# Gate recurrence between the two heads of the first attention; selection by step sums, one comparison per block, low halves split on VectorE

## The chip, the cores and the metric

The kernel runs on one core of one Trainium2 chip. The metric is the device time of one execution in microseconds (us): before the change 1979.73 us, the median of three runs (1979.67 to 1980.06). Lower is better.

Of a core's engines the kernel uses TensorE (PE: matmuls and transposes, with its weight loads as a queue of their own), VectorE (DVE), ScalarE (ACT), GpSimd (POOL) and SyncE (SP, which here only starts DMAs). Each engine takes its instructions strictly in the order in which they stand in its queue, and waits where an operand is not ready.

## What is computed

One decoder block over 512 tokens of width 1024, in float32. A normalised input goes through one combined projection. Two token mixers read it, a differential attention and an mLSTM with 8 heads each; their outputs are gated, merged and projected. Then comes a feed-forward part in which each token picks 128 of 16384 experts. Cut to what the change touches:

```python
# mLSTM: log-gates, running sums and running maxima over the tokens
log_f = log_sigmoid(f_pre);  b = cumsum(log_f);  Dm = b_j - b_k + i_k
m_j = max(max(Dm), b + m_prev);  W = exp(Dm - m_j)

# expert choice, for each token and each of 8 heads
s = einsum('thpd,hpnd->thpn', (h @ w_q), sub_keys)      # two halves of 128 scores
v_top, i_top = top_k(s, 16)
cand     = v_top[0][:, None] + v_top[1][None, :]        # sums of two scores
cand_idx = i_top[0][:, None] * 128 + i_top[1][None, :]
sc, sel  = top_k(cand, 16)
idx  = take_along_axis(cand_idx, sel)                   # expert = n1 * 128 + n2
gate = softmax(sc)

# experts
act = gelu(einsum('thed,td->the', U[idx], h))
y   = einsum('the,thed->td', gate * act, V[idx])
```

## The kernel before

A float32 product is made of three matmuls on halves: `hi` is a rounded copy (a cast, mostly on ACT), `lo` what is left over (a subtraction, `split` at L138, or L181 for the weights of a projection).

**Head pairs, about 60 to 600 us.** The loop at L667 takes the heads in four pairs `hp`. For each it calls `attention` (projections of q, k and v; then for each of the two heads `u` the scores `sc` L478 to L481, the maximum `nmx` L483, the exponential L487, `p` L492, the transposes `aTp` L495, their split, the output `po` and its transposes `pt` L507, and the scaled result `mrg` L509), then `mlstm`, then three gate projections `om`, `gm` and `ga`, each closed by sigmoids on ACT (L682). PE projects `om`, `gm` and `ga` with matmuls of 256 columns (L187 to L189). The first pair alone also calls `gate_chain`, the recurrence over the gates of all heads: on an 8-partition tile four rounds of a running maximum `M` (L349), `mprev`, `iw` and `R` (L350 to L352), then exponentials on ACT (L355 to L357), splits, and transposes `RTp` (L369). It reads two small projections made long before, and the mLSTM of every pair reads its results.

**Routing and the dense weights, about 640 to 1013 us.** `scores(h)` projects the keys of a head and takes the best 16 of each half on VectorE. `select` (called by `select_dense` with four heads of one of three token blocks, six calls, and by two later `select_gather` calls for a fourth token block) adds up to 50 candidate sums `cand` on VectorE and their indices `cidx` on GpSimd, takes the best 16, and then finds the index of each with, per head, a comparison `eq` on VectorE (L797), a product `oh` on GpSimd (L799) and a sum on VectorE (L800), over 16x50 elements. `slots` (L816) turns the indices and gates of a token block. `build_w` (L833) makes the dense gate weights of 384 tokens in 48 blocks of 8 tokens: two comparisons `onehot` (`e2`, `e1`), two products `gated` (`r_hi`, `r_lo`), each of 128x1024 fp16 (L844), on VectorE, save 6 of the 48 `r_lo`, which are on GpSimd; then 16 small matmuls into `wps` (L852, L853).

Meanwhile PE is given the first products with `U`: `up(n1)` (L961) loads a row of 128 experts, casts `hi_U` on ACT (L966), subtracts `lo_U` (L967; for n1 below 35 on GpSimd, later on VectorE), copies one column of `lo_U` on GpSimd (`pace`, L969, to pace the gathers), and issues 24 matmuls `act` (L975 to L977) and a gelu into one of 32 `ga` tiles.

**Main loop, 1013 to 1984 us.** For each of 128 rows n1: one further `up`, a load of `V` and its split, the gate weights, and 18 matmuls `y` (L1021).

The order on each engine is not the order of the code: a scheduler goes through all instructions with durations of its own and hands each engine a list. So where code is moved, the lists move around it.

Of the kernel before, what the change touches and what calls it, by code (L numbers as in the profile page):

```python
# [61 lines left out]
def block_kernel(ctx: ExitStack, tc: tile.TileContext, a, out, dbg=None):  # L62
# [709 lines left out]
    def select(vals, inds, n, mk, didx, dgate):  # L772

        fi = mk("fi", [P, 2, n, TOPK])
        A.activation(fi[:, 0], inds[:, 0], AF.Copy, scale=float(KEYS))
        A.copy(fi[:, 1], inds[:, 1])
        cand = mk("cand", [P, n, NC])
        cidx = mk("cidx", [P, n, NC])
        for eng, dst, src in ((V, cand, vals), (G, cidx, fi)):
            off = 0  # L780
            for i in range(8):
                m = PAIRS[i]
                eng.tensor_tensor(dst[:, :, off:off + m], src[:, 1, :, 0:m],
                                bc(src[:, 0, :, i:i + 1], [P, n, m]), op=OP.add)
                off += m
            eng.tensor_tensor(dst[:, :, off:off + 8], src[:, 0, :, 8:16],
                            bc(src[:, 1, :, 0:1], [P, n, 8]), op=OP.add)
# [21 lines left out]
    def mk_rp(name, shape, dt=F32):  # L809
        return rp.tile(shape, dt, tag=name, bufs=2, name=name)  # L810

    def select_dense(t, h0, n):
        hs = slice(h0, h0 + n)
        select(vals[t][:, :, hs], inds[t][:, :, hs], n, mk_rp, idxf[t][:, hs], gates[t][:, hs])

    def slots(t):  # L816
# [9 lines left out]
        pair = [P, P, 2]  # L826
        V.tensor_copy(n1T[:, cs], bc(ii[:, 1, :, None], pair))
        V.tensor_copy(n2T[:, cs], bc(ii[:, 2, :, None], pair))
        gp = bc(ps[:, P:2 * P, None], pair)
# [89 lines left out]
    def select_gather(h0):  # L919
# [5 lines left out]
        def mk(name, shape, dt=F32):  # L925
            n = int(np.prod(shape[1:])) * (2 if dt == F16 else 4) // 4
            if name in ("oh", "eq"):
# [1 line left out]
            elif name in ("cand", "cidx"):
                t_, n0 = s0, 256 * (name == "cidx")  # L930
# [178 lines left out]
```

## Time and profile before

| What | us |
|---|---|
| median of three runs | 1979.73 |
| profiled execution, its own time | 1986.29 |
| span of that execution's instructions | 1984.2 |
| busy PE / DVE / ACT / POOL | 1826.5 / 1465.3 / 806.8 / 861.2 |

The profiled execution is 6.6 us longer than the median, and 2.1 us of its own time lie outside its span. A busy time is the sum over an engine's instructions; an engine that waits within an instruction for a resource counts as busy. In a timeline, the bracket behind a row gives the idle time ahead of it and what ended it. An instruction's duration may overlap the next one's start by some 0.08 us.

### The profile page before, as it was taken

How to read it: one execution, taken by the hardware profiler on the slowest of the kernel's cores; microseconds unless marked ns; L12 is line 12 of the kernel's file. 1: busy time of each engine (PE TensorE's matmuls, PEld its weight loads, DVE VectorE, ACT ScalarE, POOL GpSimd, SP SyncE). 2: the span in 40 equal slices, each digit the busy share in tenths (PEclk: the TensorE clock that was granted, in tenths of full speed). 3: DMA queues.
4: the chain of work that ended last, by engine and by line, in shares of the span. 5: the costliest groups of instructions: out<-in, count | busy, mean ns of one | idle time of the engine just before them, and what ended most of it. 6: DMA issues, size and time to landing. Idle time of an engine off the chain costs nothing.

```text
span 1984.2 us, 29045 instructions
## 1 busy us (share of the span) xinstructions
PE 1826.5 (92%) x10748; PEld 1648.0 (83%) x10748; DVE 1465.3 (74%) x2740; ACT 806.8 (41%) x1361; POOL 861.2 (43%) x721
## 2 busy tenths in 40 slices
PE   5989999899997988778899989999999999999997
PEld 4979899798986877678888778889988888888986
DVE  7653646546557799998999878888777677767777
ACT  4545464464553323344444333333333333332332
POOL 2513425234234256675533556555433423333433
PEclk8999999999998999899899999999999999999998
DMA  7321414324223222255596699999978888887983
GB/s 278 123 64 60 149 65 154 113 67 139 64 86 107 86 90 81 85 183 202 203 312 215 216 331 339 334 345 348 337 253 296 293 283 291 288 299 234 320 290 129
DMA packets 160284, 404.27 MB, mean 204 GB/s; under 512 B 14471, under 2 KB 63368, under 8 KB 160142
## 3 DMA queue, kind: packets, MB, share of 16 engines
q1 hardware_dynamic: 117026, 240.91, 37.2%
q0 software_dynamic: 36864, 134.23, 18.6%
q10 hardware_dynamic: 6252, 27.28, 3.6%
q8 instruction: 84, 1.38, 0.3%
q14 instruction: 58, 0.48, 0.1%
HBM read 373.52 MB, written 28.84 MB: 203 GB/s over the span
## 4 chain that ended last, share of the span: by engine, by line
PE 51%; DVE 23%; DMA 10%; issue 6%; POOL 5%; ACT 4%; SPq 0%; DVEq 0%; POOLq 0%; ACTq 0%
PE y L1021 18%; PE act L977 5%; PE act L975 5%; PE act L976 5%; DMA ada_w<-ada_w 4%; DMA gath<-V,idx 3%; DVE onehot L844 3%; DVE gated L844 2%; DVE lo_V L138 1%; DVE lo_U L967 1%; DVE eq L797 1%; DMA gath<-U,idx 1%; POOL gath L901 1%; DVE idxf L800 1%; ACT hi_U L966 1%
## 5 line engine op out<-in xcount | busy, mean ns | idle before, releaser
L977 PE MATMUL act<-h_hi,lo_U 128*128 128x384 f32 x1024 | 353.9, 346 | 14.7 <-POOL lo_U L967 9.7
L975 PE MATMUL act<-h_hi,hi_U 128*128 128x384 f32 x1024 | 351.5, 343 | 1.9 <-ACT ga L979 1.9
L976 PE MATMUL act<-h_lo,hi_U 128*128 128x384 f32 x1024 | 350.7, 342 | 0.0
L917 DVE SCALAR_TENSOR_TENSOR yg<-gath,act,yg 128x1024 f32<-128x1024 f32 x127 | 162.9, 1283 | 110.3 <-DMA gath<-V,idx 109.6
L1021 PE MATMUL y<-lo_V,ahi 128*128 128x512 f32 x762 | 238.9, 394 | 5.5 <-DVE lo_V L138 5.5
L1021 PE MATMUL y<-hi_V,alo 128*128 128x512 f32 x762 | 234.1, 394 | 4.0 <-DVE alo L138 4.0
L1021 PE MATMUL y<-hi_V,ahi 128*128 128x512 f32 x762 | 222.1, 396 | 7.3 <-ACT hi_V L137 7.3
L901 POOL DMA_INDIRECT gath<-U,idx x128 | 176.6, 1380 | 115.3 <-DVE junk L907 101.1
L137 ACT CAST hi_V<-raw_V 128x1024 fp32r<-128x1024 f32 x128 | 134.1, 1051 | 225.6 <-PE y L1021 197.1
L977 PEld LDWEIGHTS act<-h_hi,lo_U 128*128 128x128 f32 x1024 | 197.0, 192 | 22.4 <-POOL lo_U L967 11.1
L969 POOL COPY pace<-lo_U 128x1 f32<-128x1 f32 x128 | 69.9, 548 | 331.6 <-DVE lo_U L967 330.1
L975 PEld LDWEIGHTS act<-h_hi,hi_U 128*128 128x128 f32 x1024 | 197.8, 193 | 10.8 <-ACT ga L979 3.1
L976 PEld LDWEIGHTS act<-h_lo,hi_U 128*128 128x128 f32 x1024 | 197.5, 193 | 3.6
L137 ACT CAST ahi<-ga 128x384 fp32r<-128x384 f32 x127 | 65.1, 513 | 302.2 <-DVE ga L1006 152.1
L138 DVE TENSOR_TENSOR lo_V<-raw_V,hi_V 128x1024 fp32r<-128x1024 f32 x128 | 158.0, 1236 | 33.2 <-ACT hi_V L137 30.6
L966 ACT CAST hi_U<-raw_U 128x1024 fp32r<-128x1024 f32 x128 | 134.1, 1048 | 110.0 <-PE act L976 92.3
L1021 PEld LDWEIGHTS y<-hi_V,alo 128*128 128x128 f32 x762 | 143.5, 189 | 35.9 <-DVE alo L138 5.2
L1021 PEld LDWEIGHTS y<-lo_V,ahi 128*128 128x128 f32 x762 | 142.7, 189 | 36.7 <-DVE lo_V L138 7.9
L1021 PEld LDWEIGHTS y<-hi_V,ahi 128*128 128x128 f32 x762 | 143.0, 190 | 32.1 <-ACT hi_V L137 8.0
L901 POOL DMA_INDIRECT gath<-V,idx x128 | 152.5, 1192 | 38.0 <-issue 30.2
L907 DVE SCALAR_TENSOR_TENSOR junk<-gath,hrow 128x1024 bf16<-128x1024 f32 x128 | 156.1, 1220 | 11.9 <-DMA gath<-U,idx 11.2
L967 POOL TENSOR_TENSOR lo_U<-raw_U,hi_U 128x1024 fp32r<-128x1024 f32 x35 | 105.0, 3001 | 72.5 <-ACT hi_U L966 59.1
(461 smaller groups left out, 4413.1 us busy)
## 6 DMA issues: line engine op xcount, KB each, us to landing
raw_U<-UT SPq DMA_DIRECT2D x128, 512.0 KB, 5.1
raw_V<-V SPq DMA_DIRECT2D x128, 512.0 KB, 5.0
ada_w<-ada_w SPq DMA_DIRECT2D x96, 256.0 KB, 4.0
W_dram<-st ACTq DMA_DIRECT2D x24, 960.0 KB, 4.5
W<-W_dram SPq DMA_DIRECT2D x60, 384.0 KB, 10.4
raw_wq<-wq SPq DMA_DIRECT2D x16, 512.0 KB, 3.5
raw_q<-w_in SPq DMA_DIRECT2D x8, 512.0 KB, 4.9
raw_k<-w_in SPq DMA_DIRECT2D x8, 512.0 KB, 3.6
```

The lines of the kernel that those rows point to most:

```text
L137: A.copy(hi, src)
L138: eng.tensor_tensor(lo, src, hi.bitcast(F32), op=OP.subtract)
L844: eng.tensor_tensor(dst.rearrange("p t (n u) -> p t n u", u=2), x.rearrange("p t (n u) -> p t n u", u=2), bc(y[:, b * TB:(b + 1) * TB, Non ...
L901: G.indirect_dma_start(out=t_, out_offset=None, in_=src, in_offset=bass.IndirectOffsetOnAxis(ap=idx0[:, s:s + 1], axis=0))
L907: V.scalar_tensor_tensor(junk2, u, 1.0, hrow, op0=OP.mult, op1=OP.mult, accum_out=act[:, s:s + 1])
L917: V.scalar_tensor_tensor(yg, v, act[:, s:s + 1], yg, op0=OP.mult, op1=OP.add)
L966: A.copy(hi, raw)
L967: (G if n1 < NGA + 3 else V).tensor_tensor(lo, raw, hi.bitcast(F32), op=OP.subtract)
L975: T.matmul(ps, hi[:, ks], h_hi[:, k], start=(k == 0), stop=False)
L976: T.matmul(ps, hi[:, ks], h_lo[:, k], start=False, stop=False)
L977: T.matmul(ps, lo[:, ks], h_hi[:, k], start=False, stop=(k == KD - 1))
L1021: T.matmul(ys[d][j], l[:, tsl], r[:, j * 512:(j + 1) * 512], start=(m == 0 and i == 0), stop=(m == KEYS - 1 and i == 2))
```

## The change

- `gate_chain` is called between head 0 and head 1 of the first pair's attention, no longer after both.
- `select` makes no index table and does nothing on GpSimd. The position of a pick is compared with the 16 offsets at which the rows of candidates start (`ge`, is-greater-or-equal, four heads at once, 1024 elements); that is multiplied by the steps of the first index (`di`) and by the steps of the offsets (`doff_c`) into the two halves of `stp`; one sum over 2048 elements gives the first index and the row's offset. The rest of the position is compared with 0 to 15 and multiplied by the second index, and summed (1024 elements). All of it is on VectorE, so a call has five elementwise operations of 1024 fp16 elements, two sums, and four small operations, where it had four comparisons and four sums on VectorE and four products on GpSimd.
- `slots` turns three tables and needs no shift or mask.
- `build_w` makes both comparisons of a block in one operation of 2048 elements, and all 48 `r_lo` are on VectorE.
- `lo_U` is on VectorE for all n1. The `pace` copy stays on GpSimd.
- The tables off_c and doff_c are filled by 32 GpSimd memsets of one column each; the two `select_gather` calls use the new `select`.

```diff
-PLO = 1
...
-    def attention(hp, y, ssq):
+    def attention(hp, y, ssq, between=None):
...
+            if u and between:
+                between()
...
-        attention(hp, y_a, ssq[:, 0])
-        if hp == 0:
-            gate_chain()
+        attention(hp, y_a, ssq[:, 0], gate_chain if hp == 0 else None)
...
+    off_c, doff_c, iota_c = [dp.tile([P, TOPK], F16, name=n) for n in ("off_c", "doff_c", "iota_c")]
...
-    def select(vals, inds, n, mk, didx, dgate):
-
-        fi = mk("fi", [P, 2, n, TOPK])
-        A.activation(fi[:, 0], inds[:, 0], AF.Copy, scale=float(KEYS))
-        A.copy(fi[:, 1], inds[:, 1])
+    def select(vals, inds, n, mk, dn1, dn2, dgate):
+
+        ij = mk("ij", [P, 2, n, TOPK], F16)
+        A.copy(ij, inds)
+        di = mk("di", [P, n, TOPK], F16)
+        V.tensor_copy(di[:, :, 0:1], ij[:, 0, :, 0:1])
+        V.tensor_tensor(di[:, :, 1:], ij[:, 0, :, 1:], ij[:, 0, :, :TOPK - 1], op=OP.subtract)
...
-        cidx = mk("cidx", [P, n, NC])
-        for eng, dst, src in ((V, cand, vals), (G, cidx, fi)):
...
-        pos2 = mk("pos2", [P, n, TOPK, 2], F16)
-        A.copy(pos2, bc(pos[:, :, :, None], [P, n, TOPK, 2]))
-        for h in range(n):
-            eq, oh = mk("eq", [P, TOPK, NC], F16), mk("oh", [P, TOPK, NC])
-            sh = [P, TOPK, NC // 2, 2]
-            V.tensor_tensor(eq.rearrange("p k (c u) -> p k c u", u=2), bc(pos2[:, h, :, None, :], sh),
-                            bc(iota_c.rearrange("p (c u) -> p c u", u=2)[:, None], sh), op=OP.is_equal)
-            G.tensor_tensor(oh, eq, bc(cidx[:, h, None, :], [P, TOPK, NC]), op=OP.mult)
-            V.tensor_reduce(didx[:, h], oh, axis=AX.X, op=OP.add)
+        pos2 = mk("pos2", [P, n * TOPK, 2], F16)
+        A.copy(pos2, bc(pos.rearrange("p h k -> p (h k)")[:, :, None], [P, n * TOPK, 2]))
+
+        sh = [P, n * TOPK, TOPK // 2, 2]
+        sh4 = [P, n, TOPK, TOPK]
+
+        def each_pos(dst, table, op):
+            V.tensor_tensor(dst.rearrange("p q (c u) -> p q c u", u=2), bc(pos2[:, :, None, :], sh),
+                            bc(table.rearrange("p (c u) -> p c u", u=2)[:, None], sh), op=op)
+
+        def of_head(dst, src, table):
+            V.tensor_tensor(dst.rearrange("p (h k) c -> p h k c", h=n), src.rearrange("p (h k) c -> p h k c", h=n),
+                            bc(table[:, :, None, :], sh4), op=OP.mult)
+        ge = mk("ge", [P, n * TOPK, TOPK], F16)
+        st = mk("stp", [P, 2 * n * TOPK, TOPK], F16)
+        two = mk("two", [P, 2, n * TOPK])
+        each_pos(ge, off_c, OP.is_ge)
+        of_head(st[:, 0:n * TOPK], ge, di)
+        V.tensor_tensor(st[:, n * TOPK:], ge, bc(doff_c[:, None, :], [P, n * TOPK, TOPK]), op=OP.mult)
+        V.tensor_reduce(two.rearrange("p a q -> p (a q)"), st, axis=AX.X, op=OP.add)
+        V.tensor_copy(dn1, two[:, 0].rearrange("p (h k) -> p h k", k=TOPK))
+        V.tensor_tensor(pos2, pos2, bc(two[:, 1, :, None], [P, n * TOPK, 2]), op=OP.subtract)
+        eq = mk("ge", [P, n * TOPK, TOPK], F16)
+        each_pos(eq, iota_c, OP.is_equal)
+        of_head(eq, eq, ij[:, 1])
+        V.tensor_reduce(dn2, eq.rearrange("p (h k) c -> p h k c", h=n), axis=AX.X, op=OP.add)
...
-        ii = rp.tile([P, TOPK * NC], I32, tag="oh", bufs=2, name="ii")[:, 0:3 * P].rearrange("p (a b) -> p a b", b=P)
-        V.tensor_copy(ii[:, 0], ps[:, 0:P])
-        V.tensor_scalar(ii[:, 1], ii[:, 0], 7, None, op0=OP.logical_shift_right)
-        V.tensor_scalar(ii[:, 2], ii[:, 0], KEYS - 1, None, op0=OP.bitwise_and)
...
-            def each(dst, x, y, op, eng=V):
-                eng.tensor_tensor(dst.rearrange("p t (n u) -> p t n u", u=2), x.rearrange("p t (n u) -> p t n u", u=2),
-                                bc(y[:, b * TB:(b + 1) * TB, None, :], sh), op=op)
-            each(e2, iota_rep, n2T, OP.is_equal)
-            each(e1, iota_rep, n1T, OP.is_equal)
-            each(r_hi, e1, ghi, OP.mult)
-            each(r_lo, e1, glo, OP.mult, G if b % 8 < PLO else V)
+            V.tensor_tensor(pairs[0].rearrange("p a t (n u) -> p (a t) n u", u=2),
+                            iota_rep.rearrange("p t (n u) -> p t n u", u=2),
+                            bc(n21T[:, b].rearrange("p a t u -> p (a t) u")[:, :, None, :], [P, 2 * TB, KEYS // 2, 2]),
+                            op=OP.is_equal)
+            V.tensor_tensor(r_hi.rearrange("p t (n u) -> p t n u", u=2), e1.rearrange("p t (n u) -> p t n u", u=2),
+                            bc(ghi[:, b * TB:(b + 1) * TB, None, :], sh), op=OP.mult)
+            V.tensor_tensor(r_lo.rearrange("p t (n u) -> p t n u", u=2), e1.rearrange("p t (n u) -> p t n u", u=2),
+                            bc(glo[:, b * TB:(b + 1) * TB, None, :], sh), op=OP.mult)
...
-        (G if n1 < NGA + 3 else V).tensor_tensor(lo, raw, hi.bitcast(F32), op=OP.subtract)
+        V.tensor_tensor(lo, raw, hi.bitcast(F32), op=OP.subtract)
```

How the lists move, at three places.

VectorE, first head pair, from the low half of the `gm` weights (`lo_gm`) and the last low halves of attention weights (`a_lo`) on; `M`, `mprev`, `iw`, `R` are the gate recurrence, `mrg` the result of a head. Before, at the end of head 1:

```order
L138 TENSOR_TENSOR a_lo<-aTp,a_hi 128x3x128
L138 TENSOR_TENSOR a_lo<-aTp,a_hi 128x4x128
L349 SCALAR_TENSOR_TENSOR M<-Gr,mprev 8x128
L350 TENSOR_TENSOR mprev<-Fc,M 8x1
L351 TENSOR_SCALAR iw<-M,mprev 8x128
L352 TENSOR_SCALAR R<-Gr,M 8x128
L349 SCALAR_TENSOR_TENSOR M<-Gr,mprev 8x128
L509 TENSOR_SCALAR mrg<-pt,rinv 128x128
```

Now, at the end of head 0:

```order
L138 TENSOR_TENSOR a_lo<-aTp,a_hi 128x3x128
L138 TENSOR_TENSOR a_lo<-aTp,a_hi 128x4x128
L181 TENSOR_TENSOR lo_gm_0_1604<-raw_gm_0_1602,hi_gm_0_1603 128x1024
L349 SCALAR_TENSOR_TENSOR M<-Gr,mprev 8x128
L350 TENSOR_TENSOR mprev<-Fc,M 8x1
L351 TENSOR_SCALAR iw<-M,mprev 8x128
L352 TENSOR_SCALAR R<-Gr,M 8x128
```

The recurrence stands one head earlier, ahead of head 0's `mrg` instead of between those of head 1.

PE, head 1 of the first pair. Before, the last scores and transposes, then the output, then the `gm` projection:

```order
L480 MATMUL sc<-kT_hi,qz_643 128x512
L481 LDWEIGHTS identb
L481 MATMUL sc<-mask_qk,identb 128x128
L495 MATMUL aTp<-ident,p 128x128 x9
L187 MATMUL po<-a_hi,v_hi 128x512
```

Now the transposes of the same head stand within the `ga` projection, whose first half `pt_ga_0` this is, behind all of `gm`:

```order
L188 MATMUL pt_ga_0_1738<-lo_ga_4_1734,hT_hi 128x256
L497 MATMUL aTp<-ident,p 128x128 x3
L189 MATMUL pt_ga_0_1738<-hi_ga_4_1733,hT_lo 128x256
L187 MATMUL pt_ga_0_1738<-hi_ga_0_1727,hT_hi 128x256
L188 MATMUL pt_ga_0_1738<-lo_ga_0_1728,hT_hi 128x256
```

Between the steps of head 1 PE has matmuls of the gate projections, which before came only behind the head's output.

PE, end of the weight blocks. Before, the last block is followed by products with `U` (`act`):

```order
L852 LDWEIGHTS onehot
L852 MATMUL wps<-gated,onehot 128x128
L853 LDWEIGHTS onehot
L853 MATMUL wps<-gated,onehot 128x128
L976 MATMUL act<-h_lo,hi_U_11622 128x384
L977 MATMUL act<-h_hi,lo_U_11623 128x384
```

Now it is followed by the first products with `V`:

```order
L871 LDWEIGHTS onehot
L871 MATMUL wps<-gated,onehot 128x128
L872 LDWEIGHTS onehot
L872 MATMUL wps<-gated,onehot 128x128
L1041 MATMUL y_0_9172<-hi_V_9218,ahi 128x512
L1041 MATMUL y_1_9173<-hi_V_9218,ahi 128x512
```

Counted over the lists, PE has done 9.0 rows of `U` ahead of the first block before the change and 14.1 after it, 33.1 and 34.0 ahead of the first `y`; and in the new list the last 13 of the 48 blocks have no product with `U` between them.

## Rows read from the trace of the kernel before

**Rows 1.** Busy time by engine in stretches of the run: start and end, length, then busy us (number of instructions) of PE, PE's weight loads, DVE, ACT, POOL, the granted TensorE clock as a share of full speed, DMA share, GB/s. The stretch from 1003.5 to 1013.3 lies between the last product of the last weight block on DVE and the first `y`.

```profile
130.00:160.00 30.00, 17.59 (x83) 14.25 (x84) 17.09 (x45) 16.52 (x39) 5.09 (x4) 0.72 0.12 40
...
690.00:752.00 62.00, 56.96 (x267) 47.12 (x267) 58.80 (x297) 17.81 (x35) 33.33 (x42) 0.97 0.28 86
752.00:810.00 58.00, 43.74 (x223) 41.79 (x222) 54.64 (x280) 22.44 (x38) 40.50 (x52) 0.88 0.28 87
810.00:1003.50 193.50, 159.50 (x1315) 150.02 (x1315) 180.65 (x213) 83.95 (x142) 117.85 (x60) 0.91 0.52 183
1003.50:1013.30 9.80, 9.80 (x69) 9.49 (x68) 7.33 (x6) 4.90 (x9) 6.43 (x4) 1.00 0.69 239
...
1160.00:1960.00 800.00, 788.64 (x3902) 706.05 (x3901) 606.91 (x742) 276.16 (x379) 357.84 (x325) 1.00 0.86 301
```

**Rows 2.** What PE waited for from 50 to 230 us, by its line and the releaser: us in total, times, longest.

```profile
PE pt_gm L187 <- ACT om L682: 6.6, 1, 6.6
PE aTp L495 <- DVE p L492: 4.3, 3, 2.4
```

**Rows 3.** ACT in order of time at the end of head 1 of the first pair: start, us, line, operation.

```profile
150.84 1.28 ACT L682 ACT_TABLE_LOAD   x1
152.13 1.08 ACT L682 ACTIVATE om<-pt_om 128x512 f32<-128x512 f32 x2
```

**Rows 4.** PE in order of time, the `gm` projection behind head 1: two neighbouring matmuls just after the wait, two of the same kind 6 us later.

```profile
153.16 0.42 PE L188 MATMUL pt_gm<-lo_gm,hT_hi 128*128 128x256 f32 x1
153.38 0.41 PE L189 MATMUL pt_gm<-hi_gm,hT_lo 128*128 128x256 f32 x1
...
158.82 0.28 PE L187 MATMUL pt_gm<-hi_gm,hT_hi 128*128 128x256 f32 x1
158.94 0.28 PE L188 MATMUL pt_gm<-lo_gm,hT_hi 128*128 128x256 f32 x1
```

**Rows 5.** DVE in order of time at the end of head 0 of the first pair.

```profile
119.72 0.35 DVE L509 TENSOR_SCALAR mrg<-pt,rinv 128x128 f32<-128x128 f32 x1 [5.56 <-PE pt L507]
```

**Rows 6.** DVE's work from 707 to 1003.5 us in groups by line and shape: number, busy us, mean ns of one, idle time ahead and its releaser.

```profile
L844 DVE TENSOR_TENSOR onehot<-iota,n2T 128x1024 f16<-128x1024 f16 x48 | 51.0, 1067 | 12.6 <-PE wps L853 12.6
L844 DVE TENSOR_TENSOR gated<-onehot,ghi 128x1024 f16<-128x1024 f16 x48 | 47.2, 990 | 0.2
L844 DVE TENSOR_TENSOR onehot<-iota,n1T 128x1024 f16<-128x1024 f16 x48 | 45.7, 955 | 0.0
L844 DVE TENSOR_TENSOR gated<-onehot,glo 128x1024 f16<-128x1024 f16 x42 | 34.6, 824 | 0.0
L797 DVE TENSOR_TENSOR eq<-pos,iota_c 128x800 f16<-128x800 f16 x24 | 24.1, 1015 | 0.0
L800 DVE TENSOR_REDUCE idxf<-oh 128x16 f32<-128x800 f32 x24 | 23.2, 968 | 0.0
L783 DVE TENSOR_TENSOR cand<-vals 128x64 f32<-128x64 f32 x5 | 7.3, 1464 | 0.0
...
L138 DVE TENSOR_TENSOR lo_wq<-raw_wq,hi_wq 128x1024 fp32r<-128x1024 f32 x2 | 2.4, 1212 | 0.0
...
L802 DVE TENSOR_TENSOR ex<-scs 128x64 f32<-128x64 f32 x6 | 1.8, 295 | 0.0
```

**Rows 7.** DVE in order of time within the weight blocks.

```profile
829.34 0.68 DVE L844 TENSOR_TENSOR onehot<-iota,n1T 128x1024 f16<-128x1024 f16 x1
...
837.33 0.98 DVE L800 TENSOR_REDUCE idxf<-oh 128x16 f32<-128x800 f32 x1
838.23 1.86 DVE L797 TENSOR_TENSOR eq<-pos,iota_c 128x800 f16<-128x800 f16 x1
...
840.61 2.14 DVE L844 TENSOR_TENSOR onehot<-iota,n1T 128x1024 f16<-128x1024 f16 x1
...
843.88 2.88 DVE L844 TENSOR_TENSOR onehot<-iota,n2T 128x1024 f16<-128x1024 f16 x1
```

**Rows 8.** POOL in order of time in the same stretch.

```profile
837.27 2.39 POOL L967 TENSOR_TENSOR lo_U<-raw_U,hi_U 128x1024 fp32r<-128x1024 f32 x1 [7.81 <-issue]
839.72 0.41 POOL L969 COPY pace<-lo_U 128x1 f32<-128x1 f32 x1
840.09 2.11 POOL L799 TENSOR_TENSOR oh<-eq,cidx 128x800 f32<-128x800 f16 x1
843.32 2.89 POOL L967 TENSOR_TENSOR lo_U<-raw_U,hi_U 128x1024 fp32r<-128x1024 f32 x1 [1.12 <-ACT hi_U L966]
```

**Rows 9.** POOL's work from 707 to 1003.5 us in groups by line and shape, columns as in Rows 6.

```profile
L967 POOL TENSOR_TENSOR lo_U<-raw_U,hi_U 128x1024 fp32r<-128x1024 f32 x32 | 97.3, 3041 | 66.3 <-ACT hi_U L966 52.9 <-issue 7.8 <-ACT W L858 5.1
L799 POOL TENSOR_TENSOR oh<-eq,cidx 128x800 f32<-128x800 f16 x24 | 45.6, 1907 | 25.7 <-DVE eq L797 19.1 <-DVE n2T L828 4.5 <-DVE vals L750 0.9
```

**Rows 10.** What PE waited for from 690 to 1130 us, columns as in Rows 2.

```profile
PE wps L852 <- DVE gated L844: 17.0, 8, 5.2
PE act L977 <- POOL lo_U L967: 9.7, 5, 4.3
```

**Rows 11.** The ends of the stretch: PE in order of time, two neighbouring products with `U`; DVE in order of time, the last product of the last block.

```profile
1000.21 0.34 PE L977 MATMUL act<-h_hi,lo_U 128*128 128x384 f32 x1
1000.39 0.34 PE L975 MATMUL act<-h_hi,hi_U 128*128 128x384 f32 x1
...
1002.77 0.69 DVE L844 TENSOR_TENSOR gated<-onehot,glo 128x1024 f16<-128x1024 f16 x1
```

More of the change, by code (lines that the diff above doesn't have):

```diff
@@ L37 @@
 NC = sum(PAIRS)
+OFFS = [sum(PAIRS[:i]) for i in range(TOPK)]
 PIECES = [c for hp in range(4) for c in (
@@ L738, in block_kernel @@
     V.tensor_copy(iota16, jcol)
-    iota_rep = bc(iota16[:, None, :], [P, TB, KEYS])
-    V.tensor_copy(iota_c, jcol[:, 0:NC])
+    iota_rep = bc(iota16[:, None, :], [P, 2 * TB, KEYS])
+    V.tensor_copy(iota_c, jcol[:, 0:TOPK])
+    for i in range(TOPK):
+        G.memset(off_c[:, i:i + 1], float(OFFS[i]))
+        G.memset(doff_c[:, i:i + 1], float(OFFS[i] - OFFS[max(i - 1, 0)]))
     vals, inds = [{t: rp.tile([P, 2, NH, TOPK], dt, name=f"{n}{t}") for t in DBS}
                   for n, dt in (("vals", F32), ("inds", U32))]
-    idxf, gates = [{t: rp.tile([P, NH, TOPK], F32, name=f"{n}{t}") for t in DBS} for n in ("idxf", "gates")]
+    picks = {t: rp.tile([P, 3, NH, TOPK], F32, name=f"picks{t}") for t in DBS}
     def top16(src, scratch, v, i):
@@ L770, in scores @@
         A.dma_start(s0_dram[:, h], s0)
-    def select(vals, inds, n, mk, didx, dgate):
-        fi = mk("fi", [P, 2, n, TOPK])
-        A.activation(fi[:, 0], inds[:, 0], AF.Copy, scale=float(KEYS))
-        A.copy(fi[:, 1], inds[:, 1])
-        cand = mk("cand", [P, n, NC])
-        cidx = mk("cidx", [P, n, NC])
-        for eng, dst, src in ((V, cand, vals), (G, cidx, fi)):
[L780 to L787, printed above, removed]
+    def select(vals, inds, n, mk, dn1, dn2, dgate):
[4 more added lines that the diff above has]
+        V.tensor_tensor(di[:, :, 1:], ij[:, 0, :, 1:], ij[:, 0, :, :TOPK - 1], op=OP.subtract)
+        cand = mk("cand", [P, n, NC])
+        off = 0
+        for i in range(8):
+            m = PAIRS[i]
+            V.tensor_tensor(cand[:, :, off:off + m], vals[:, 1, :, 0:m], bc(vals[:, 0, :, i:i + 1], [P, n, m]), op=OP.add)
+            off += m
+        V.tensor_tensor(cand[:, :, off:off + 8], vals[:, 0, :, 8:16], bc(vals[:, 1, :, 0:1], [P, n, 8]), op=OP.add)
         sc = mk("scs", [P, n, TOPK])
@@ L809, in mk_rp @@
     def mk_rp(name, shape, dt=F32):
-        return rp.tile(shape, dt, tag=name, bufs=2, name=name)
+        return rp.tile(shape, dt, tag=name, bufs=1 if name == "stp" else 2, name=name)
     def select_dense(t, h0, n):
         hs = slice(h0, h0 + n)
-        select(vals[t][:, :, hs], inds[t][:, :, hs], n, mk_rp, idxf[t][:, hs], gates[t][:, hs])
+        select(vals[t][:, :, hs], inds[t][:, :, hs], n, mk_rp, *[picks[t][:, i, hs] for i in range(3)])
     def slots(t):
         cs = slice((t - DBS[0]) * P, (t - DBS[0] + 1) * P)
+        bs = slice((t - DBS[0]) * P // TB, (t - DBS[0] + 1) * P // TB)
         ps = tr_tile("slots")
-        T.transpose(ps[:, 0:P], idxf[t].rearrange("p h k -> p (h k)"), ident)
-        T.transpose(ps[:, P:2 * P], gates[t].rearrange("p h k -> p (h k)"), ident)
-        ii = rp.tile([P, TOPK * NC], I32, tag="oh", bufs=2, name="ii")[:, 0:3 * P].rearrange("p (a b) -> p a b", b=P)
-        V.tensor_copy(ii[:, 0], ps[:, 0:P])
-        V.tensor_scalar(ii[:, 1], ii[:, 0], 7, None, op0=OP.logical_shift_right)
-        V.tensor_scalar(ii[:, 2], ii[:, 0], KEYS - 1, None, op0=OP.bitwise_and)
[L826 to L829, printed above, removed]
+        for i in range(3):
+            T.transpose(ps[:, i * P:(i + 1) * P], picks[t][:, i].rearrange("p h k -> p (h k)"), ident)
+        for i in range(2):
+            src = ps[:, i * P:(i + 1) * P].rearrange("p (b t) -> p b t", t=TB)
+            V.tensor_copy(n21T[:, bs, 1 - i], bc(src[:, :, :, None], [P, P // TB, TB, 2]))
+        gp = bc(ps[:, 2 * P:3 * P, None], [P, P, 2])
         V.tensor_scalar(ghi[:, cs], gp, GS, None, op0=OP.mult)
@@ L926, in mk @@
             n = int(np.prod(shape[1:])) * (2 if dt == F16 else 4) // 4
[L927 removed]
+            if name in ("ge", "stp"):
                 t_, n0 = gpool.tile([P, D], F32, tag="g", bufs=NGB, name=name), 0
[L929 to L930 removed]
+            elif name == "cand":
+                t_, n0 = s0, 0
             else:
```

11 lines of the change are left out of this document (6 added, 5 removed).

## The prediction

> **What bounds the kernel now.** I read the stretches first [rows 1]. In the main loop PE works 788.6 of 800 us at the full granted clock: nothing is to be had there, and the change touches little in it. PE leaves time in two places that the change touches. From 130 to 160 us it works 17.6 of 30 us, at a granted clock of 0.72. From 690 to 1003.5 us it is idle for 5.0 + 14.3 + 34.0 = 53.3 us, while DVE works 58.8 + 54.6 + 180.7 = 294.1 of 313.5 us. So the weight stage is bound by DVE, and what PE waits for there is DVE's last product of a block (17.0 us) and GpSimd's `lo_U` (9.7 us) [rows 10]. Its end is DVE's: the last `gated` is over at 1003.5 [rows 11].
>
> Then I looked at what DVE does in those 294 us, because a busy DVE need not be working. The same 128x1024 comparison takes 0.68 us at 829.34 and 2.14 and 2.88 at 840.61 and 843.88 [rows 7]. Against GpSimd's timeline [rows 8] the long ones begin where a GpSimd product or subtraction runs (840.09 to 842.20, 843.32 to 846.21) and end 0.5 us behind it: DVE is held for GpSimd's instruction and then does its own 0.6 us. The sum at 837.33 takes its usual 0.98 though `lo_U` started at 837.27, so it isn't held; the `eq` behind it is. Over the stretch the four block operations take 51.0 + 47.2 + 45.7 + 34.6 = 178.5 us for 186 instructions, a mean of 0.96 [rows 6]; at 0.68 it would be 126.5. So 52 us of DVE's busy time is waiting for GpSimd.
>
> **The gate recurrence.** Before, PE has only head 1's softmax to work on and then waits: 6.6 us for `om`, whose sigmoid comes late on ACT, 4.3 for `p` [rows 2]; the sigmoid stands behind the recurrence's exponentials and a table load of 1.28 [rows 3]. Idle in the window: 30.0 - 17.6 = 12.4. After the wait PE runs slowly, a matmul each 0.22 us for about 5 us (22 steps) instead of each 0.12 [rows 4]: 2.2 more. Together 14.6. Now the recurrence stands at the end of head 0, where DVE waited 5.6 us for `pt` [rows 5], and head 1 of the first pair has the `gm` and `ga` projections between its steps, as the order shows: each of them is 96 matmuls of 0.12, 11.5 us, more than any single wait. What is late next is ACT: it gets exponentials and sigmoids in turns, and by the functions in its list three more table loads, 3 x 1.28 = 3.8 us [rows 3], in a stretch where it works 16.5 of 30 [rows 1]. That fits, barely, and I leave some 1.6 us for it: **-13**. Bounds: all of 14.6 and 2 more for the end of the mLSTM, -17; or half of it given back to ACT, -5.
>
> The Trainium skill ("ScalarE: Activation LUTs", section "What ACT_TABLE_LOAD costs") gives such a switch about 1.28 us of load and 1.38 us of drain. In the trace the next activation starts 0.01 us behind the load's end (150.84 + 1.28 to 152.13) [rows 3], so a drain does not show here. By the page three switches would be 8.0 us of ACT and the gain some 4 us less.
>
> **The weight stage, on DVE's list.** Taken away, at the price without GpSimd: 24 sums, 23.2 [rows 6]; 24 `eq` of 800 elements at 0.68 x 800/1024 = 0.53, 12.7; casts, shift and mask of the indices, an estimate of 2; two comparisons in one save the start of one, and as 0.68 holds an overlap of 0.08, 48 x 0.08 = 3.8. Sum 41.7.
>
> Added: `lo_U` of 34 rows at the price of the same subtraction on DVE, 1.21 (`lo_wq`) [rows 6]: 41.1. Six `r_lo` at 0.68: 4.1. Six calls of `select`, each five operations of 1024 at 0.68 (3.4), a sum of 2048 at 0.97/800 an element (2.5), one of 1024 (1.2), small ones 0.5: 7.6, in all 45.6. Sum 90.8. If a sum over fp16 went twice as fast as one over float32 it would be 11 less; no row shows one, and I take the rate that I have. So at bare prices DVE gets **49 us more**.
>
> Given back by GpSimd, which keeps no work here but one-column copies: 52.0 on the block operations; 24.1 - 12.7 = 11.4 on `eq`; on `cand` 7.3 less 5 x 0.30 (the price of a 128x64 operation alone, `ex`) = 5.8; on the other small ones, an estimate, 2.8. Sum **72**. The 34 `pace` copies remain, at most 0.41 each [rows 8] of which some hit a block operation: +3. Net 49 - 72 + 3 = -20.
>
> The Trainium skill ("SBUF — State Buffer", section "Who interferes with whom") states the rule: a DVE instruction with two SBUF inputs and a GpSimd instruction that reads SBUF hold each other up entirely, whoever came first. The trace agrees (2.88 instead of 0.68, and a sum with one input that is not held). By it the `pace` copies, which read SBUF, can still hold `lo_U` and the blocks, and that speaks against a full return.
>
> At the end of the stage two things are better. The first `y` followed the last block after 9.8 us, all of them PE's work [rows 1], because products with `U` stood in between; now `y` stands right behind it, about 3 less. And 0.9 more rows of `U` are done by then, 24 x 0.18 = 4.3 us each [rows 11]: -3.8. Stage: **-27**. The memsets of the tables lie on GpSimd long before; the selection for the fourth block is in the main loop, where DVE has a fourth of its time free [rows 1]: no term, at most 6 either way. PE can follow: its 270 us of work there hold matmuls at a clock of 0.88 to 0.97, and 43 us less of waiting is to be had; but the last 13 blocks are bare, 13 x (1.28 + 1.36) = 34 us in which PE has 12 us of small matmuls, so not all of its 53 us can go.
>
> **Sum.** 1986.3 for the profiled execution - 13 - 27 = 1946; its median stood 6.6 lower, so 1979.7 - 40 = **1940**.
>
> **The rivals.**
> - A, the gain is larger: sums at twice the rate (-11) and PE filled up to its bare tail (another -10 or so from the 53 idle us): 1979.7 - 13 - 50 = 1915 or so. For it: DVE's list is all that PE waits for. Against it: the tail.
> - B, DVE takes over GpSimd's waits. GpSimd's `lo_U` waited 66 us in the stretch, 53 of it for `hi_U` [rows 9], which ACT makes when PE frees a buffer. On DVE's list such a wait holds all blocks queued behind it, and PE then waits for them. If some 20 us of it land on DVE, the stage gives only 0 to 8: 1979.7 - 13 - 4 = 1962. For it: the list has 34 such places. Against it: the scheduler put them with the buffers in mind, and GpSimd had time to run ahead and wait, where DVE has not.
> - C, the recurrence gives back: ACT is the bound with its extra loads, and head 1's output comes late: -2 instead of -13, 1951.
> - D, slower. The long block operations are not GpSimd's doing, or the remaining copies and DMA starts hold DVE as often. Then DVE has 49 us more and little relief: 1979.7 + 49 - 13 - 3 = 2013 with none. It decides for slower from the point where less than 30 of the 72 us come back. Against it: start and end of the long ones follow GpSimd's instructions to 0.5 us, in each case that I followed. That the recurrence only moves and nothing else works is within this case.
>
> **How the numbers follow.** Forecast (1925 to 1955) 0.54; A 0.13; B 0.18; C 0.07; D 0.08. The range 1917 to 1967 holds the forecast, B, C and the near part of A; outside lie D and the far half of A. About 0.2% (4 us) is what a measurement of this kernel can tell from no change. Faster by more than that: all of A, C and the forecast, and B but for the case in which the recurrence gives back too: 0.88. Within: 0.04. Slower: 0.08.
>
> **What the profile after would show.** Right: 130 to 160 us with PE over 27 us busy and a clock near 1; 128x1024 block operations at a mean near 0.70, comparisons of 2048 near 1.3; the last `gated` some 35 us earlier, of which 13 from the first pair; DVE busy without gaps. Wrong: DVE idle ahead of `lo_U` for `hi_U` (B); block operations still near 0.95 (D); PE waiting for `om` or `a_hi` in the first pair (C); a sum of 2048 at 1.3 (towards A). A granted clock well under 0.9 in the last 34 us of the stage would cost up to 12 us on its small matmuls only where PE, not DVE, ends last.

## The result, and the profile after

The changed kernel takes 1922.89 us (median of 4 runs, 1921.88 to 1928.04) against 1979.89 for the kernel before: a ratio of 0.9713 with an interval of 0.9692 to 0.9734, 53 to 61 us faster. 1940 was forecast, with a range of 1917 to 1967: the sign and the range held, the gain was 57 and not 40. Run again beside other kernels (below) the ratio was 0.9725 (0.9702 to 0.9749).

The profiled execution of the changed kernel took 1921.88, its span is 1920.1. The stretches that answer to [rows 1]; all that stands behind the first head pair comes 13 us earlier, so 677 to 959.4 here answers to 690 to 1003.5 there, and 1110 to 1890 lies in the main loop (columns as there):

```profile
130.00:160.00 30.00, 27.41 (x200) 25.26 (x199) 16.85 (x28) 22.69 (x43) 12.08 (x8) 0.94 0.24 75
...
937.00:963.20 26.20, 15.90 (x161) 13.44 (x161) 24.90 (x33) 14.24 (x26) 11.79 (x1) 0.70 0.69 247
...
1110.00:1890.00 780.00, 775.11 (x3833) 690.57 (x3833) 593.84 (x720) 270.98 (x370) 337.19 (x320) 1.00 0.87 305
...
677.00:959.40 282.40, 261.02 (x1893) 239.57 (x1892) 271.71 (x791) 128.85 (x216) 64.98 (x40) 0.96 0.50 171
959.40:963.20 3.80, 0.26 (x6) 0.09 (x3) 3.44 (x5) 2.84 (x6) 0.00 (x0) 0.67 0.45 86
```

The window of the recurrence now has PE at 27.4 of 30 us and a granted clock of 0.94, where it had 17.6 and 0.72. In the weight stage GpSimd works 65 us, PE is idle for 21 us instead of 53, and DVE still works 96% of the time: it stays the bound, on a shorter list.

DVE's groups from its first candidate sums to the last product, 694.4 to 958.2 us, in the columns of [rows 6]:

```profile
L861 DVE TENSOR_TENSOR onehot<-iota,n21T 128x2048 f16<-128x2048 f16 x48 | 57.2, 1215 | 2.8 <-PE wps L872 2.8
L987 DVE TENSOR_TENSOR lo_U<-raw_U,hi_U 128x1024 fp32r<-128x1024 f32 x36 | 43.7, 1213 | 1.0 <-ACT hi_U L986 0.6 <-issue 0.4
L865 DVE TENSOR_TENSOR gated<-onehot,ghi 128x1024 f16<-128x1024 f16 x48 | 32.5, 681 | 0.2
L867 DVE TENSOR_TENSOR gated<-onehot,glo 128x1024 f16<-128x1024 f16 x48 | 32.5, 681 | 0.0
L815 DVE TENSOR_REDUCE two<-stp 128x128 f32<-128x2048 f16 x6 | 13.6, 2267 | 0.0
...
L821 DVE TENSOR_REDUCE picks<-ge 128x64 f32<-128x1024 f16 x6 | 7.2, 1203 | 0.0
...
L789 DVE TENSOR_TENSOR cand<-vals 128x64 f32<-128x64 f32 x5 | 1.5, 299 | 0.0
```

Every product of a block takes 0.68 us, the bare price; 122 us for the blocks where there were 178. GpSimd in the same stretch:

```profile
L989 POOL COPY pace<-lo_U 128x1 f32<-128x1 f32 x36 | 55.3, 1541 | 165.2 <-DVE lo_U L987 165.2
```

The one-column copies lengthen to 1.54 us, and no DVE group shows it: now it is GpSimd that is held. What PE waits for from 640 to 964 us, and from 50 to 230 us, against [rows 10] and [rows 2]:

```profile
PE wps L871 <- DVE gated L865: 6.1, 7, 2.0
PE act L995 <- ACT ga L999: 5.4, 3, 2.8
PE y L1041 <- ACT ahi L137: 3.5, 1, 3.5
...
PE act L997 <- DVE lo_U L987: 2.5, 3, 0.9
```

```profile
PE sc L481 <- DVE kT_lo L138: 3.1, 2, 1.7
PE sc L480 <- ACT p L489: 1.5, 1, 1.5
```

GpSimd's `lo_U` is gone from the one, `om` from the other, and the longest wait for a block's product is 2.0 us where it was 5.2.

Where the time went, by two marks on PE in each profiled execution (the start of the last of the first head's eight key-score matmuls, and of the first `y`), in us; they stand in these rows, before and after:

```profile
657.95 1.16 PE L764 MATMUL pkeys<-keysT,qt 128*128 128x128 f32 x8
...
1013.23 0.63 PE L1021 MATMUL y<-hi_V,ahi 128*128 128x512 f32 x2
```

```profile
644.83 1.16 PE L770 MATMUL pkeys<-keysT,qt 128*128 128x128 f32 x8
...
963.19 0.79 PE L1041 MATMUL y<-hi_V,ahi 128*128 128x512 f32 x1 [3.54 <-ACT ahi L137]
```

| Kernel | to the first key scores | from there to the first y | from there to the end |
|---|---|---|---|
| before | 658.8 | 354.4 | 971.0 |
| after | 645.7 | 317.5 | 956.9 |
| e1 recurrence alone | 647.4 | 355.9 | 964.4 |
| e2 lo_U alone | 654.9 | 332.5 | 979.7 |
| e3 lo_U back on GpSimd | 646.8 | 341.0 | 963.7 |
| e4 old selection | 646.0 | 328.7 | 972.8 |
| e5 GpSimd products added | 648.3 | 344.0 | 957.2 |
| e6 GpSimd memsets added | 647.8 | 318.6 | 962.9 |
| e7 two comparisons | 647.4 | 322.9 | 958.8 |
| e8 one product | 646.0 | 314.4 | 965.3 |
| e9 changed kernel again | 646.3 | 318.8 | 959.3 |
| e10 old selection in the loop alone | 643.5 | 318.0 | 972.7 |
| e11 33 ga tiles | 647.7 | 317.2 | 948.2 |
| e12 both | 645.1 | 316.9 | 951.4 |

Of before and after the three parts differ by 13.1, 36.9 and 14.1, in all 64; by medians it is 57, because the profiled execution of before lay 6.6 above its median and that of after 1.0 below. Kernels that share a part differ in it by some 4 us in the first part and 1.5 in the second (before and e1; after, e9 and e10). In the last they differ by some 8 with the new selection (after, e3 and e5 to e9) and by 15 with the old one (before, e1 and e2; longest in e2, though it has one row of U more done by then), so much is wander between executions or comes from how the lists happen to lie. The 7 us that the medians lack are therefore most likely in the last part, which leaves some 7 of its 14; that is an estimate from these figures and no measurement.

### The profile page after: what moved, and what is told of

It reads as the page before. It is cut to its first block, busy times and chain, and to the rows that moved or that the text cites. A ratio compares the mean times of both kernels' runs of the same rounds, so it can differ in the third digit from the quotient of the medians.

```text
span 1920.1 us, 28920 instructions
## 1 busy us (share of the span) xinstructions
PE 1815.4 (95%) x10751; PEld 1631.7 (85%) x10751; DVE 1431.1 (75%) x2748; ACT 813.1 (42%) x1359; POOL 686.5 (36%) x608
## 4 chain that ended last, share of the span: by engine, by line
PE 61%; DVE 18%; DMA 7%; ACT 6%; issue 4%; POOL 3%; SPq 0%; DVEq 0%; POOLq 0%; ACTq 0%
PE y L1041 22%; PE act L997 7%; PE act L995 7%; PE act L996 7%; DMA gath<-V,idx 3%; DMA ada_w<-ada_w 3%; DVE lo_U L987 1%; DVE ada_acc L219 1%; POOL gath L920 1%; DVE ga L699 1%; DVE lo_V L138 1%; ACT p L489 1%; ACT hi_U L986 1%; PE pr_wq L187 1%; PE wps L872 1%
## 5 line engine op out<-in xcount | busy, mean ns | idle before, releaser
L997 PE MATMUL act<-h_hi,lo_U 128*128 128x384 f32 x1024 | 346.6, 339 | 5.7 <-DVE lo_U L987 5.5
L995 PE MATMUL act<-h_hi,hi_U 128*128 128x384 f32 x1024 | 345.7, 338 | 6.4 <-ACT ga L999 5.4
L996 PE MATMUL act<-h_lo,hi_U 128*128 128x384 f32 x1024 | 344.8, 337 | 0.0
L989 POOL COPY pace<-lo_U 128x1 f32<-128x1 f32 x128 | 103.3, 809 | 570.5 <-DVE lo_U L987 570.3
L995 PEld LDWEIGHTS act<-h_hi,hi_U 128*128 128x128 f32 x1024 | 193.0, 188 | 12.9 <-ACT ga L999 6.7
L997 PEld LDWEIGHTS act<-h_hi,lo_U 128*128 128x128 f32 x1024 | 192.7, 188 | 12.9 <-DVE lo_U L987 8.9
L996 PEld LDWEIGHTS act<-h_lo,hi_U 128*128 128x128 f32 x1024 | 192.7, 188 | 3.9
L987 DVE TENSOR_TENSOR lo_U<-raw_U,hi_U 128x1024 fp32r<-128x1024 f32 x128 | 155.9, 1219 | 22.7 <-ACT hi_U L986 21.2
```

The lines of the kernel that those rows point to most:

```text
L987: V.tensor_tensor(lo, raw, hi.bitcast(F32), op=OP.subtract)
L989: with tc.issue_after(G.tensor_copy(pace, lo[:, 0:1].bitcast(F32)).ins):
L995: T.matmul(ps, hi[:, ks], h_hi[:, k], start=(k == 0), stop=False)
L996: T.matmul(ps, hi[:, ks], h_lo[:, k], start=False, stop=False)
L997: T.matmul(ps, lo[:, ks], h_hi[:, k], start=False, stop=(k == KD - 1))
```

## The experiments

All ratios are to the kernel before, run beside it on the same chip; its runs lay between 1973 and 1990 us there, so ratios are compared, not times. e1 to e4, e5 to e8 and e9 to e12 ran on three chips, and the changed kernel itself only beside the last four. e6, e7 and e8, in which little should move, all came out 5 to 10 us above it by the ratios, so a difference of that size between the groups says nothing.

**e1, the recurrence alone.** The kernel before with

```diff
...
-        attention(hp, y_a, ssq[:, 0])
-        if hp == 0:
-            gate_chain()
+        attention(hp, y_a, ssq[:, 0], gate_chain if hp == 0 else None)
```

> The kernel before, with the gate recurrence between the two heads and nothing else. Theory (the predicted term): 13 us faster, 1967, with PE over 27 of 30 us busy from 130 to 160 us and everything behind it only shifted. Rival (in the changed kernel the first pair only gains because other lists moved too): within 4 us of 1980.

Measured: 0.9942 (0.9916 to 0.9967), 7 to 17 us faster. The first part is 11.4 shorter, the stage behind it as long as before, and from 130 to 160 us PE works 27.6 of 30. The recurrence's term is confirmed; the rival is out.

**e2, lo_U alone.** The kernel before with

```diff
-        (G if n1 < NGA + 3 else V).tensor_tensor(lo, raw, hi.bitcast(F32), op=OP.subtract)
+        V.tensor_tensor(lo, raw, hi.bitcast(F32), op=OP.subtract)
```

> The kernel before, with lo_U of all rows on DVE and nothing else; the index products oh and six r_lo stay on GpSimd. Theory (DVE's two-input operations are held by GpSimd's): DVE gets 34 x 1.21 = 41 us, and is relieved by lo_U's share of the 72 us, 97 of the 159 us that lo_U, oh and r_lo take on GpSimd, so 44, and of some of its 13 us of idle time: 1965 to 1980, with block operations at a mean near 0.8. Rival (the long ones are not GpSimd's doing): 41 us more on the bounding list, 2015 to 2025, block operations still at 0.96.

Measured: 0.9942 (0.9919 to 0.9965), 7 to 16 us faster, within the theory's bounds. DVE's groups from 640 to 1014 us:

```profile
L967 DVE TENSOR_TENSOR lo_U<-raw_U,hi_U 128x1024 fp32r<-128x1024 f32 x36 | 47.9, 1330 | 0.3
L844 DVE TENSOR_TENSOR onehot<-iota,n1T 128x1024 f16<-128x1024 f16 x48 | 37.8, 792 | 0.0
L844 DVE TENSOR_TENSOR gated<-onehot,ghi 128x1024 f16<-128x1024 f16 x48 | 36.1, 751 | 0.2
L844 DVE TENSOR_TENSOR onehot<-iota,n2T 128x1024 f16<-128x1024 f16 x48 | 34.8, 728 | 0.6 <-PE wps L853 0.6
```

DVE took on 48 us and yet the stage is 22 us shorter: block operations fell from a mean of 0.96 to 0.75, and the 12.6 us for which DVE waited for `wps` [rows 6] fell to 0.6. Work added to the bounding engine made the stage shorter. The last part is 9 us longer (979.7 against 971.0), within its wander, so the whole run shows less than the stage.

**e3, lo_U back.** The changed kernel with that one line as before.

> The changed kernel, with lo_U of the first 35 rows back on GpSimd and nothing else; the scheduler moves the lists. Theory: DVE loses 41 us of its own work and is held for 35 subtractions of 2.4 to 2.9 us for about half of the time, +44, and PE waits for GpSimd's lo_U as before, +10: 1930 to 1950, block operations near 0.85. Rival (no hold): 41 us less on DVE's list, 1885 to 1905, block operations at 0.68.

Measured: 0.9849 (0.9809 to 0.989), some 25 to 27 us slower than the changed kernel, at the upper end of what the theory said. Without the 41 us of `lo_U` DVE's list still became slower:

```profile
L861 DVE TENSOR_TENSOR onehot<-iota,n21T 128x2048 f16<-128x2048 f16 x48 | 71.6, 1525 | 11.8 <-PE wps L872 11.7
L865 DVE TENSOR_TENSOR gated<-onehot,ghi 128x1024 f16<-128x1024 f16 x48 | 53.6, 1120 | 0.1
L867 DVE TENSOR_TENSOR gated<-onehot,glo 128x1024 f16<-128x1024 f16 x48 | 39.1, 819 | 0.0
```

Blocks cost 42 us more, DVE waits 11.7 for PE again, and PE 12.8 for GpSimd's `lo_U`:

```profile
PE act L997 <- POOL lo_U L987: 12.8, 6, 5.2
```

**e4, the old selection.** The changed kernel with the old `select`; its table of indices goes into the merged comparison (the edit of `slots`, against the kernel before):

```diff
-        V.tensor_copy(n1T[:, cs], bc(ii[:, 1, :, None], pair))
-        V.tensor_copy(n2T[:, cs], bc(ii[:, 2, :, None], pair))
+        bs = slice((t - DBS[0]) * P // TB, (t - DBS[0] + 1) * P // TB)
+        for i in range(2):
+            src = ii[:, 1 + i].rearrange("p (b t) -> p b t", t=TB)
+            V.tensor_copy(n21T[:, bs, 1 - i], bc(src[:, :, :, None], [P, P // TB, TB, 2]))
```

> The changed kernel with the old selection (eq and sums per head on DVE, oh and the index table on GpSimd); recurrence, merged comparison, r_lo and lo_U as changed. Theory: DVE's bare list is 8 to 11 us shorter (23 + 13 + 2 against 47), and it is held for 24 products oh of 1.9 us for about half of the time, +21: 1930 to 1940. Rival (the step sums cost more than they free): 1912 to 1916.

Measured: 0.9844 (0.9799 to 0.9889), some 24 to 26 us slower than the changed kernel, more than the theory's 7 to 17. Only 11 of it lie in the stage, as the theory had it; 16 lie behind the first `y`, where the theory had nothing. That led to e10.

**e5, GpSimd reads.** The changed kernel with, for the first 32 rows of U,

```diff
+            G.tensor_copy(dummy[:, 0:1], lo[:, 0:1].bitcast(F32))
+            for _ in range(5):
+                G.tensor_tensor(dummy, dummy, dummy, op=OP.mult)
```

> The changed kernel with five more GpSimd instructions behind each of the first 32 lo_U, products of a 128x200 float32 tile of its own with itself, which nothing else reads. Theory (a GpSimd instruction that reads SBUF holds DVE's two-input operations and is held by them): 160 instructions of some 0.5 us each are 80 us on GpSimd, of which about half falls on DVE: block operations at a mean of 0.8 or more, DVE's sums unchanged, 20 to 40 us slower, 1943 to 1963. Rival (the old stalls came from what GpSimd computed, not from its running): within 4 us of 1923, block operations at 0.68.

Measured: 0.9854 (0.9826 to 0.9881), some 26 to 28 us slower than the changed kernel, all of it in the stage (344.0 against 317.5). In order of time on DVE, then on GpSimd:

```profile
885.16 0.68 DVE L867 TENSOR_TENSOR gated<-onehot,ghi 128x1024 f16<-128x1024 f16 x1
885.77 1.00 DVE L869 TENSOR_TENSOR gated<-onehot,glo 128x1024 f16<-128x1024 f16 x1
886.69 1.53 DVE L989 TENSOR_TENSOR lo_U<-raw_U,hi_U 128x1024 fp32r<-128x1024 f32 x1
```

```profile
885.36 6.16 POOL L994 TENSOR_TENSOR dummy<-dummy 128x200 f32<-128x200 f32 x5
```

A DVE operation that meets one of these products takes 0.32 us more, 1.00 for 0.68 and 1.53 for 1.21, and five products take 6.16 us, since each waits for a DVE operation in turn: the shortest of the 160 takes 0.51 us, the mean is 0.92. The sums over `stp` are at 2.265, untouched. The group of products (its shortest, median and longest in ns, then its busy time and mean) and that of the sums:

```profile
L994 POOL TENSOR_TENSOR dummy<-dummy x160: 514/848/2222, 743.5 to 948.6; 128x200 f32<-128x200 f32 x160
L994 POOL TENSOR_TENSOR dummy<-dummy 128x200 f32<-128x200 f32 x160 | 147.0, 919 | 10.3
...
L817 DVE TENSOR_REDUCE two<-stp 128x128 f32<-128x2048 f16 x6 | 13.6, 2265 | 0.0
```

Nothing reads what the products write, so it is GpSimd's running that holds DVE.

**e6, GpSimd writes.** The same with `G.memset(dummy, 0.0)` in place of the product.

> The same with five memsets of that tile in place of the five products: GpSimd writes and does not read. Theory with the rule that only GpSimd's reads hold DVE: within 4 us of 1923 and block operations at 0.68. Rival (every GpSimd instruction on SBUF holds DVE): as the run with products, in proportion to the memsets' length.

Measured: 0.9751 (0.9718 to 0.9784), whose interval overlaps that of the changed kernel in either measurement. The groups in the stage, on DVE and on GpSimd:

```profile
L863 DVE TENSOR_TENSOR onehot<-iota,n21T 128x2048 f16<-128x2048 f16 x48 | 57.3, 1218 | 3.5 <-PE wps L874 3.5
...
L867 DVE TENSOR_TENSOR gated<-onehot,ghi 128x1024 f16<-128x1024 f16 x48 | 32.6, 683 | 0.2
```

```profile
L994 POOL MEMSET dummy<- 128x200 f32 x160 | 42.3, 265 | 7.5
```

160 memsets lengthen nothing; the stage is 318.6, as in the changed kernel. They are shorter than the products (42 us in all against 147), but a hold in proportion would be 8 us, and no group shows any.

**e7, two comparisons,** and **e8, one product.** The changed kernel with the block's comparison in two operations, and with its two products in one:

```diff
-            V.tensor_tensor(pairs[0].rearrange("p a t (n u) -> p (a t) n u", u=2),
...
+            for i in range(2):
+                V.tensor_tensor(pairs[0][:, i].rearrange("p t (n u) -> p t n u", u=2),
+                                iota_rep[:, 0:TB].rearrange("p t (n u) -> p t n u", u=2),
+                                bc(n21T[:, b, i][:, :, None, :], sh), op=OP.is_equal)
```

```diff
-            V.tensor_tensor(r_hi.rearrange("p t (n u) -> p t n u", u=2), e1.rearrange("p t (n u) -> p t n u", u=2),
...
+            V.tensor_tensor(pairs[1].rearrange("p a t (n u) -> p a t n u", u=2),
+                            bc(e1.rearrange("p t (n u) -> p t n u", u=2)[:, None], [P, 2] + sh[1:]),
+                            bc(ghl[:, b][:, :, :, None, :], [P, 2] + sh[1:]), op=OP.mult)
```

> The changed kernel with the comparison of a block as two operations of 1024 elements, as before. By the bare prices 48 x 0.08 = 4 us more on DVE: 1926 to 1927. Rival (the block's comparison lies beside PE's work): within 2 us of 1923.

> The changed kernel with a block's two products also in one operation of 2048 elements, the table of gates laid out as the one of indices. If the step from two to one saves as much as for the comparison, 48 x 0.08 = 4 us less on DVE: 1919. Rival (an operand with four dimensions goes at a lower rate, or the stage's end is no longer DVE's): 1923 or more.

Measured: 0.9757 (0.9732 to 0.9783) and 0.9762 (0.9738 to 0.9786); both intervals overlap that of the changed kernel run again, so neither forecast, 4 us more and 4 us less, is decided by the whole run; e8 came out slower by the ratio, not faster. In the traces the stage is 4 to 5 us longer for e7 and 3 to 4 shorter for e8, and the 48 comparisons take 61.0 us in two against 57.2 in one: the bare prices, too small to show in the time of a whole run. The comparisons of e7:

```profile
L862 DVE TENSOR_TENSOR onehot<-iota,n21T 128x1024 f16<-128x1024 f16 x96 | 61.0, 682 | 3.2 <-PE wps L872 2.8
```

**e9 to e12.** The changed kernel again; with the old selection in the two `select_gather` calls alone (a second copy of the old function under another name, called there, with its own table of 50 columns); with 33 `ga` tiles; and the last together with e8.

```diff
-        select(vals0, inds0, 4, mk, idg, idl, gate0[:, gs].rearrange("p (h k) -> p h k", k=TOPK))
+        select_old(vals0, inds0, 4, mk, idg, gate0[:, gs].rearrange("p (h k) -> p h k", k=TOPK))
```

```diff
-NGA = 32
+NGA = 33
...
-        return rp.tile(shape, dt, tag=name, bufs=1 if name == "stp" else 2, name=name)
+        return rp.tile(shape, dt, tag=name, bufs=1 if name in ("stp", "ge") else 2, name=name)
```

> The changed kernel itself, to stand beside the three others on the same chip: 1923, 57 us below the kernel before.

> The changed kernel with the old selection in the two calls for the fourth token block alone (index table and products on GpSimd, within the main loop). Theory (the 14 us by which the trace after is shorter behind the first y come partly from the new selection there): 5 to 10 us slower, 1928 to 1933, with 5 to 10 us of PE idle in the stretch from 60 to 180 us behind the first y, as before. Rival (that part is the wander of the loads from one execution to the next): within 3 us of the control, and the idle time comes and goes.

> The changed kernel with 33 instead of 32 ga tiles, so that PE makes one more row of products with U ahead of the first y (the order shows 35 instead of 34); ge has one buffer to make room. Theory (PE has 22 us idle in the stage and DVE's list sets its end): 4.3 us less in the loop for 1.2 us more on DVE, 3 us faster than the control. Rival (the 13 bare blocks are no room, since the added row stands ahead of them and PE ends last): no gain.

> One operation for the two products of a block, and 33 ga tiles. If both save what their bare prices say (the products 3 us in the stage's length in the trace of the run with them alone), 5 to 6 us faster than the control; the loop's wander is of that size.

Measured: 0.9725 (0.9702 to 0.9749), 0.9822 (0.9801 to 0.9844), 0.9721 (0.9701 to 0.9742), 0.9705 (0.9683 to 0.9728). The intervals of e9 and e10 lie apart: in the changed kernel the selection of the fourth block costs 16 us more in its old form by the medians (1941.18 against 1925.47) and 19 by the ratios, above what the theory gave. From 60 to 180 us behind the first `y`, two stretches each of e9 and then of e10 (columns as in [rows 1]):

```profile
1025.10:1085.10 60.00, 58.87 (x271) 49.54 (x270) 54.20 (x166) 26.06 (x36) 14.15 (x11) 1.00 0.63 199
1085.10:1145.10 60.00, 60.00 (x284) 51.74 (x283) 55.95 (x85) 22.59 (x30) 41.83 (x32) 1.00 0.98 377
```

```profile
1021.50:1081.50 60.00, 53.54 (x239) 43.47 (x238) 55.13 (x154) 23.89 (x33) 25.05 (x23) 1.00 0.44 132
1081.50:1141.50 60.00, 53.67 (x243) 45.82 (x242) 46.03 (x68) 19.17 (x26) 33.33 (x26) 0.94 0.93 339
```

With the old selection PE is idle for 12.8 us there, against 1.1, and does 73 matmuls less. What it waits for in the first 180 us, of e10:

```profile
PE y L1079 <- DVE lo_V L138: 10.4, 9, 2.2
PE y L1079 <- ACT hi_V L137: 5.2, 1, 5.2
```

In e9 those two are 2.8 and 1.1. The longest single wait in e10, 5.2 us for `hi_V`, goes back to a load: ACT's cast had waited 13.3 us for its row of `V`.

```profile
1095.64 1.04 ACT L137 CAST hi_V<-raw_V 128x1024 fp32r<-128x1024 f32 x1 [13.29 <-DMA raw_V<-V]
```

e11 and e12 are not shown to be faster than the changed kernel: 1 and 4 us by the ratios, with intervals of some 4 us to either side. Their traces have the one more row of U and a last part that is 8 to 11 us shorter than in e9, but these profiled executions lay 9 and 3 us below their medians, so much of that is wander; what a row gains these runs don't resolve.

## Why the prediction was right, and where its size was off

**The recurrence: right.** -13 was forecast; the first part is 13.1 shorter in the profile and e1 gives 7 to 17. PE works 27.4 of 30 us, over the 27 that was named. ACT took three more table loads in the first pair (13 instead of 10) and bore them, so case C did not come. The drain that the prediction weighed, by which the gain would have been 4 us less, does not show in this trace either: the next activation starts at once behind a load.

```profile
121.32 1.28 ACT L682 ACT_TABLE_LOAD   x1
122.61 0.60 ACT L682 ACTIVATE om<-pt_om 128x512 f32<-128x512 f32 x1
```

**DVE held by GpSimd: right, and shown.** e5 makes the hold with work that nothing needs, e2 and e3 take it away and bring it back with the same line, and e6 shows GpSimd instructions that only write and hold nothing. Case D is out. Of the prices, the sum over 2048 elements was put at 2.5 and took 2.27, a call of `select` 7.6 and took 7.9 (its groups add to 47 us for six), `lo_U` 1.21 and took 1.21, the blocks 127 and took 122. Sums over fp16 don't go twice as fast, which was half of case A: 1024 elements more cost 1.06 us.

**The stage: mechanism right, size short.** -20 on DVE's list and -3 at the first `y` were forecast for this stretch (the 0.9 row of U shows behind it); it became 37 shorter. The missing 14: DVE's waits for `wps` fell from 12.6 [rows 6] to 2.8 us, and the sum had left them standing (10); the `pace` copies, put at +3, cost DVE nothing (3); the gap ahead of `y` is 4.6 us (from the last block's product, over at 958.6, to 963.2) and not 7 (2). These make 15, one more than is missing. It is much of what case A had as its other half, PE's idle time going (another 10): that half came, while the sums at twice the rate did not. Case B had it that DVE would wait for `hi_U` as GpSimd did; it waits 0.6 us for it in the stage. When e3 gives `lo_U` back, GpSimd waits 112 us for `hi_U`: the wait belonged to GpSimd's place and did not move with the work.

**The loop: a term put at nothing that was not nothing.** The prediction said of the selection for the fourth block that it lies where DVE has a fourth of its time free, "no term, at most 6 either way". That share is a mean over 800 us; the two calls stand at rows 3 and 5, where DVE works 54 of 60 us in e9 and 55 in e10, and `lo_V` of the next rows is queued behind them. The first 180 us behind the first `y`, before and after (columns as in [rows 1]):

```profile
1013.20:1073.20 60.00, 58.21 (x282) 50.83 (x281) 56.65 (x169) 22.11 (x33) 19.16 (x17) 1.00 0.92 294
1073.20:1133.20 60.00, 56.47 (x259) 47.43 (x258) 56.02 (x159) 24.79 (x34) 26.82 (x27) 1.00 0.53 174
1133.20:1193.20 60.00, 54.12 (x257) 47.59 (x256) 45.76 (x70) 19.16 (x27) 33.10 (x27) 0.94 0.95 336
```

```profile
963.20:1023.20 60.00, 57.06 (x259) 48.63 (x260) 48.68 (x167) 20.15 (x30) 1.84 (x3) 0.96 0.91 285
1023.20:1083.20 60.00, 58.97 (x272) 49.67 (x272) 54.36 (x168) 26.57 (x36) 13.84 (x11) 1.00 0.61 197
1083.20:1143.20 60.00, 60.00 (x283) 51.62 (x282) 56.02 (x84) 22.37 (x30) 39.51 (x32) 1.00 0.98 378
```

PE is idle for 11.2 us of them before and 4.0 after, so in these executions the new selection is worth some 7 us. With the 3.8 for the row of U that makes 11 of the 14 of the last part, and more than the medians leave to it. e10 shows a larger price, 16 to 19 us on the whole run and 13 in the traces, but that is what the old selection costs in the changed kernel, where PE is idle for 15.7 of the 180 us (3.9 in e9), and not what the change gained by dropping it. Whether it really costs more there than in the kernel before, and why, is open. So is by which part of the old selection `lo_V` comes late: DVE's own comparisons and sums are about as long in both forms (14.4 us in e10, 14.0 in e9), so the products and index sums on GpSimd between them, their hold (`lo_U` takes 1.40 us in e10 and 1.21 in e9) and their latency, are what differs, but they weren't tried apart.

The last 10 of the 13 bare blocks, from 937.0 us on, have the granted clock at 0.70 and PE at 15.9 of 26.2 us; DVE works 24.9 there, so the low clock costs nothing beyond DVE's list, as the prediction had it. Its 12 us of PE's work for all 13, for which it showed no row, were too few.
